# Attention weights copied within SBUF and transposed as fp32r, with the transposes and the value products two items behind their scores

## The chip, the cores and the metric

The kernel runs on one core of a Trainium2 chip. The metric is the device time of one execution in microseconds (us); lower is better. Before the change the median of three runs is 2031.01 us (2028.89 to 2032.45). A difference under about 0.2% (4 us) can't be told from no change here.

## The reference

One encoder layer is applied to two sequences of 1024 tokens and width 1024 (a prompt and a sample), and then a final RMS norm. Each token is normalised, scaled and shifted, and projected to a query latent (256), a key/value latent (128), a rotary key (64) and 512 Fourier channels. Four attention heads and a 2-D Fourier transform run side by side; their outputs share one projection, and a SwiGLU feed-forward part with 2816 hidden units follows. The part that the change touches is the softmax and the product with the values:

```python
sc = (jnp.einsum('bqhd,bkhd->bhqk', qn_b, k_nope)
      + jnp.einsum('bqhr,bkr->bhqk', qp_b, k_pe)).astype(jnp.float32) * scale
p = jax.nn.softmax(sc, axis=-1).astype(v.dtype)
return jnp.einsum('bhqk,bkhd->bqhd', p, v)
```

## The kernel before

**Arithmetic.** All data is fp32. Large products run on TensorE in the type fp32r. A number is split into a rounded high part, made by a copy on ScalarE, and the rest, made by a subtraction on VectorE (`split`, L61 to L63). A product is then three matmuls: high by high, high by low, low by high (`mm3`, L82 to L85).

**Stages.** The program runs through input projections, Fourier transforms, attention with the output projection and the second norm, and then the feed-forward part. The attention stage is one loop (from L1296) over 64 items and four closing steps. An item is one sequence `s`, one block `b` of 256 tokens, one head `h` and one half `u` of 128 query rows: 2 x 4 x 4 x 2. One pass `k` of the loop does, in the order of the program text:

- `scores` of item `k`: the product with the 1024 keys into two PSUM banks, the row maximum on VectorE (L1206), its scaling to a bias `nb` (L1207), the exponential with its sum on ScalarE (L1209), the reciprocal (L1210) and the scaling of the 128 x 1024 tile `p` (L1211). Two pairs of banks take turns. `p` has three buffers.
- on some passes, work on the queries: the rotary part for the next block (`rope_q`, `rope_flip`), and the absorbed query of the next head (`absorb_q`). Their tiles `hv` (two buffers) and `qa` (three buffers) are in the pool `e`.
- on every fourth pass (`k % 4 == 1`) `values`: 24 matmuls of the last four items' transposed weights with the values.
- `flip_p` of item `k - 1`: eight 128 x 128 transposes of `p` on TensorE, in the type fp32, four to a PSUM bank, and each bank split to fp32r parts `pt`. Two banks (`tbank`) take turns; the transposes of the normalised rows (`flip_h`, tile `pht`) and of the rotary queries (`rope_flip`, tile `pqt`) use the same two.
- `out_step`, which spreads the output projection, the second norm and its transposes of an earlier block over the passes.
- small jobs from the table `todo`, such as loading and splitting the output weights (`wv_load`, `wv_split`).

**What sets the order.** The text gives each instruction a rank. A planner with a model of the instructions' costs then writes the order of each engine's queue: among the instructions that it believes ready, the one that stands first in the text goes first. So in the trace a group of transposes often stands in the middle of a later item's score product. Once written, each queue runs strictly in its order, and an instruction whose input is late holds up all that is behind it. SyncE (SP) issues nearly all DMAs and is such a queue too. The rotary transposes of L858 read fp32r tiles already; those of L1157 and L1225 read fp32.

Of the kernel before, what the change touches and what calls it, by code (L numbers as in the profile page):

```python
# [12 lines left out]
F32 = mybir.dt.float32  # L13
F32R = mybir.dt.float32r
# [7 lines left out]
P = 128  # L22
D = 1024
N = 1024
# [28 lines left out]
def hybrid_encoder_kernel(ctx: ExitStack, tc: tile.TileContext, a: dict):  # L53
    nc = tc.nc
# [3 lines left out]
    def rd(t):  # L58
        return t.bitcast(F32)

    def split(hi, lo, src):  # L61
        here["a"] = nc.scalar.copy(hi, src).ins  # L62
        here["v"] = nc.vector.tensor_tensor(out=lo, in0=src, in1=rd(hi), op=ALU.subtract).ins  # L63
# [27 lines left out]
    ident = const.tile([P, P], F32, name="ident")  # L91
    make_identity(nc, ident)
    identr = const.tile([P, P], F32R, name="identr")
# [81 lines left out]
    with ExitStack() as st:  # L175
        p1b = st.enter_context(ExitStack())
        w2 = p1b.enter_context(tc.tile_pool(name="p1b", bufs=1, side="right", reuse_waits="tile"))
        w = st.enter_context(tc.tile_pool(name="p1", bufs=1, reuse_waits="tile"))
# [617 lines left out]
    S = {}  # L796
# [9 lines left out]
            nc.gpsimd.dma_start(fo_d[s][bs, gs], xs[s][bs, gs], accum_op=ALU.add)  # L806

    def half(name):
        return e.tile([P, 512], F32, tag="hv", name=name, bufs=2)

    def load_seq(s, lat):
        ckv = [e.tile([P, 8, KVL], F32R, tag=f"ckv{i}", name=f"ckv{i}", bufs=1) for i in range(2)]
# [16 lines left out]
        return e.tile([P, HEADS, P], F32R, tag="qp", name="qp", bufs=4)  # L829

    def qa_tiles():
        return [e.tile([P, 256], F32R, tag=f"qa{i}", name=f"qa{i}", bufs=3) for i in range(2)]

    def rope_q(s, b, u, bankf):
        ql = S["q", s, b]
# [57 lines left out]
    with ExitStack() as st:  # L893
        early = st.enter_context(ExitStack())
        wa = early.enter_context(tc.tile_pool(name="p2a", bufs=1, reuse_waits="tile"))
        w = st.enter_context(tc.tile_pool(name="p2", bufs=1, side="right", reuse_waits="tile"))
# [175 lines left out]
        for s in range(2):  # L1072
            for n in range(8):
                g, j = n // 4, (1, 2, 3, 0)[n % 4]
# [14 lines left out]
                if s == 1 and n == 0:  # L1089
# [3 lines left out]
                    e = E3.enter_context(tc.tile_pool(name="p3e", bufs=1, side="left", reuse_waits="tile"))  # L1093
# [20 lines left out]
    def tbank(name, dt=F32):  # L1114
        return tl_ps.tile([P, 4, P], dt, tag="t", name=name, bufs=2)
# [48 lines left out]
    def out_step(s, b, i):  # L1164
        if i in (9, 11):
            out_load(s, b, i // 2 - 4)
        if i in (10, 12, 15, 16):
            n = (10, 12, 15, 16).index(i)
            out_proj(s, b, n // 2, n % 2)
        if i in (12, 16):  # L1170
            norm2(s, b, i // 4 - 3, tl, True)
        if i in (14, 19):
            flip_h(s, b, int(i == 19))

    with ExitStack() as st:
# [7 lines left out]
        def scores(s, b, h, u):  # L1183
            lat = S[s][0]
            qa, qp = S["qa", s, b, h], S["qp", s, b, u]
            us = slice(u * P, u * P + P)
            ps = score_bank() if u == 0 else S.pop("ps")
            for g in range(2):
                gs = slice(512 * g, 512 * g + 512)
                o = ps[:, gs]  # L1190
                nc.tensor.matmul(o, qa[0][:, us], lat[0][:, 0, gs], start=u == 0, stop=False)
                nc.tensor.matmul(o, qa[0][:, us], lat[1][:, 0, gs], start=False, stop=False)
                nc.tensor.matmul(o, qa[1][:, us], lat[0][:, 0, gs], start=False, stop=False)
                nc.tensor.matmul(o, qp[:, h, :], lat[0][:, 1, gs], start=False, stop=u == 1)
            if u == 0:
                pn, qn = score_bank(), S["qp", s, b, 1]
                for g in range(2):
                    gs = slice(512 * g, 512 * g + 512)
                    nc.tensor.matmul(ps[:, gs], qp[:64, h, :], lat[1][:64, 1, gs], start=False, stop=True)
                    nc.tensor.matmul(pn[:, gs], qn[64:, h, :], lat[1][64:, 1, gs], start=True, stop=False)  # L1200
                S["ps"] = pn
            mx = tiny.tile([P, 1], F32, name="mx")
            nb = tiny.tile([P, 1], F32, name="nb")
            sm = tiny.tile([P, 1], F32, name="sm")
            rr = tiny.tile([P, 1], F32, name="rr")
            nc.vector.tensor_reduce(out=mx, in_=ps, axis=AX.X, op=ALU.max)  # L1206
            here["nb"] = nc.vector.tensor_scalar(out=nb, in0=mx, scalar1=-SCALE, scalar2=None, op0=ALU.mult).ins  # L1207
            p = w.tile([P, N], F32, tag="p", name="p", bufs=3)
            here["exp"] = nc.scalar.activation(p, ps, AF.Exp, bias=nb, scale=SCALE, accum_out=sm).ins  # L1209
            nc.vector.reciprocal(rr, sm)  # L1210
            nc.vector.tensor_scalar(out=p, in0=p, scalar1=rr[:, 0:1], scalar2=None, op0=ALU.mult)  # L1211
            S["p", s, b, h, u] = p
            S["rr"] = rr

        def flip_p(s, b, h, u):
            p = S.pop(("p", s, b, h, u))
            if h % 2 == 0 and u == 0:
                S["pt", s, b, h // 2] = [[w.tile([P, 4, 4, P], F32R, tag=f"pt{k}{g}", name=f"pt{k}{g}", bufs=1) for k in range(2)]
                                         for g in range(2)]
            i = 2 * (h % 2) + u  # L1220
            for g in range(2):
                pth, ptl = S["pt", s, b, h // 2][g]
                pt = tbank("ppt")
                for c in range(4):
                    nc.tensor.transpose(pt[:, c, :], p[:, (4 * g + c) * P : (4 * g + c + 1) * P], ident)  # L1225
                split(pth[:, :, i, :], ptl[:, :, i, :], pt)

        def values(s, b, q):
            ckv = S[s][1]
            pts = S.pop(("pt", s, b, q))  # L1230
            if q == 0:
                S["o", s, b] = [tl.tile([P, HEADS, 256], F32R, tag=f"o{i}", name=f"o{i}b{s}{b}", bufs=3) for i in range(2)]
            o = [t[:, 2 * q : 2 * q + 2, :].rearrange("p h t -> p (h t)") for t in S["o", s, b]]
            po = gbank()
            for c in range(8):
                pth, ptl = (t[:, c % 4].rearrange("p i t -> p (i t)") for t in pts[c // 4])
                mm3(po, ckv[0][:, c, :], ckv[1][:, c, :], pth, ptl, c == 0, c == 7)
            split(o[0], o[1], po)

        items = [(s, b, h, u) for s in range(2) for b in range(4) for h in range(HEADS) for u in range(2)]  # L1240
        nit = len(items)
# [31 lines left out]
        def wv_split(i):  # L1273
            h, g = i % 4, i // 4
            gs = slice(512 * g, 512 * g + 512)
            with tc.issue_after(here["nb"]), tc.issue_after(here["exp"]):
                split(wv[0][:, h, gs], wv[1][:, h, gs], S.pop(("wv", h, g)))

        todo = {k: [] for k in range(nit)}
# [3 lines left out]
            todo[34 + 3 * g].append(lambda g=g: gate_half(1, g))  # L1283
            todo[34 + 3 * g].append(lambda g=g: wv_load(1, g))
        for i in range(8):
            todo[39 + i // 2].append(lambda i=i: wv_split(i))
            todo[3 + i].append(lambda i=i: wv_split(i))
        for c, k in enumerate((49, 51, 57, 59)):
            todo[k].append(lambda c=c: comb_h(0, c))
# [6 lines left out]
        for k in range(nit + 4):  # L1296
            if k >= nit:
                i = k - nit
                out_proj(1, 2, i // 2, i % 2)
                S["tail", i] = here["v"]  # L1300
                if i == 1:
                    norm2(1, 2, 0, tl)
                    S["tail", 5], S["tail", 6] = here["n"]
            if k < nit:
                s, b, h, u = items[k]
                scores(s, b, h, u)
                if "scale" in S:
                    with tc.issue_after(here["nb"]):
                        S.pop("scale")()
                if k == nit - 1:  # L1310
                    with tc.issue_after(here["exp"]):
                        nc.scalar.activation(tiny.tile([P, 1], F32, tag="pc", name="warm"), cmask[:, 0:1], AF.Silu)
                nxt = items[k + 8 - k % 8] if k + 8 - k % 8 < nit else None
                i = k % 8
                if nxt is not None:
                    if i == 0:
                        load_q(*nxt[:2])
                    if i == 3 and nxt[1] == 0:
                        load_seq(nxt[0], [w.tile([P, 2, N], F32R, tag=f"lat1{i}", name=f"lat1{i}") for i in range(2)])
                    if i in (3, 4):  # L1320
                        rope_q(*nxt[:2], i - 3, gbank)
                    if i in (5, 6):
                        rope_flip(*nxt[:2], i - 5, tbank("pqt", F32R))
                if u == 1 and k + 1 < nit:
                    absorb_q(*items[k + 1][:3], gbank)
            if (k % 4 == 1 and 5 <= k < nit) or k == nit + 2:
                values(*divmod(k // 8 - (k % 8 == 1), 4), k // 4 % 2 ^ 1) if k < nit else values(1, 3, 1)
                if k == nit + 2:
                    S["tail", 4], S["tail", 7] = here["v"], here["a"]
            if 0 <= k - 1 < nit:  # L1330
                flip_p(*items[k - 1])
                if k == nit:
                    S["tail"] = here["a"], here["v"]
            for n in (k // 8 - 1, k // 8 - 2):
                if 0 <= n < NOUT:
                    out_step(*divmod(n, 4), k - 8 * n)
            for f in todo.get(k, ()):
                f()

# [640 lines left out]
```

## Time and profile before

| what | value |
|---|---|
| median of three runs | 2031.01 us |
| the profiled execution's own time | 2031.3 us |
| its span, first to last instruction | 2029.5 us |
| mean granted TensorE clock | 0.994 |
| DMA traffic | 370.33 MB, 182 GB/s on average |

The time of the profiled execution is 1.8 us longer than its span and 0.3 us longer than the median. The attention stage lies between about 302 and 722 us of the span. Matmul durations in the profile overlap, because matmuls are pipelined: what one of them costs is read from the distance between the starts of neighbours, not from its own duration. The engines are TensorE (PE, and its weight loads PEld), VectorE (DVE), ScalarE (ACT), GpSimd (POOL) and SyncE (SP, shown as SPq).

### The profile page before, as it was taken

The page shows a single profiled execution, that of the slowest core. Times are in us where ns is not written, and L with a number is a line of the kernel's source. Part 1 is how long each engine was busy: PE and PEld are TensorE (multiplying, and loading weights), DVE is VectorE, ACT ScalarE, POOL GpSimd, SP SyncE. Part 2 cuts the span into 40 slices and gives each one's busy share as a digit, 9 for nine tenths or more (in the row PEclk, how much of TensorE's full clock was granted, in tenths as well). Part 3 has the DMA queues.
Part 4 walks back from the last instruction along what each step waited for, and adds up shares of the span by engine and source line. Part 5 has one row for each costly group of instructions (what it writes and reads, how often), then busy time and mean ns, then how long its engine had stood idle before and what let it go on. Part 6 is the DMA issues. An engine that isn't in the chain of part 4 may idle for free.

```text
span 2029.5 us, 28291 instructions
## 1 busy us (share of the span) xinstructions
PE 1984.2 (98%) x9840; PEld 1624.1 (80%) x9840; DVE 1407.3 (69%) x2088; ACT 896.9 (44%) x1733; POOL 830.1 (41%) x1013
## 2 busy tenths in 40 slices
PE   8899999999999999999999999999999999999997
PEld 7788877888777777888888888877788888888876
DVE  5667757766677679878677577687755655657674
ACT  4555545555555564333333365453333333336441
POOL 2454123112313227879779411233654555510142
PEclk9999999999999999999999999999999999999999
DMA  9685793445542575645655587674422322357662
GB/s 376 207 289 171 255 346 102 125 94 130 138 122 94 178 269 187 207 163 192 206 166 190 178 304 249 219 234 147 141 93 102 116 93 103 116 184 270 229 224 89
DMA packets 181963, 370.33 MB, mean 182 GB/s; under 512 B 18556, under 2 KB 58236, under 8 KB 177724
## 3 DMA queue, kind: packets, MB, share of 16 engines
q1 hardware_dynamic: 163148, 310.71, 45.8%
q0 software_dynamic: 18672, 57.81, 9.5%
q8 instruction: 77, 1.26, 0.3%
q14 instruction: 66, 0.54, 0.1%
HBM read 256.46 MB, written 120.39 MB: 186 GB/s over the span
## 4 chain that ended last, share of the span: by engine, by line
PE 54%; DVE 2%; DMA 2%; POOL 1%; issue 1%; ACT 1%; SPq 0%; DVEq 0%; ACTq 0%; POOLq 0%
PE bank L84 18%; PE bank L83 18%; PE bank L85 18%; DVE wl L63 1%; DMA draw<-s_d 1%; POOL val L143 1%; DVE val L143 1%; ACT wh L62 0%; DMA val<-x_d 0%; DMA draw<-t_d 0%; DVE val L1777 0%; POOL rs_y L110 0%; DMA rgu<-in_wgu_dram 0%; DVE val L1751 0%; DVE val L140 0%
## 5 line engine op out<-in xcount | busy, mean ns | idle before, releaser
L83 PE MATMUL bank<-H,wh 128*128 128x512 f32 x1224 | 477.3, 390 | 5.1 <-DVE val L143 5.1
L85 PE MATMUL bank<-H,wl 128*128 128x512 f32 x1224 | 476.3, 389 | 0.2 <-DVE wl L63 0.2
L84 PE MATMUL bank<-H,wh 128*128 128x512 f32 x1224 | 476.2, 389 | 0.0
L143 DVE TENSOR_TENSOR val<-bank,val 128x512 f32<-128x512 f32 x244 | 166.8, 688 | 169.9 <-PE bank L85 167.2
L83 PEld LDWEIGHTS bank<-H,wh 128*128 128x128 f32 x1224 | 229.8, 188 | 55.6 <-DVE val L143 7.0
L85 PEld LDWEIGHTS bank<-H,wl 128*128 128x128 f32 x1224 | 229.8, 188 | 49.2 <-DVE wl L63 1.1
L84 PEld LDWEIGHTS bank<-H,wh 128*128 128x128 f32 x1224 | 229.8, 188 | 47.3
L63 DVE TENSOR_TENSOR wl<-draw,wh 128x512 fp32r<-128x512 f32 x286 | 201.3, 739 | 83.0 <-ACT wh L62 82.4
L62 ACT CAST wh<-draw 128x512 fp32r<-128x512 f32 x286 | 168.6, 621 | 157.9 <-PE bank L84 86.8
L84 PE MATMUL bank<-wl,wh 128*128 128x512 f32 x572 | 223.6, 391 | 2.5 <-DVE wl L63 2.5
L143 POOL TENSOR_TENSOR val<-val 128x512 f32<-128x512 f32 x58 | 83.1, 1441 | 344.9 <-DVE val L1751 188.7
L85 PE MATMUL bank<-wh,wl 128*128 128x512 f32 x572 | 222.6, 389 | 0.0
L83 PE MATMUL bank<-wh 128*128 128x512 f32 x572 | 222.6, 389 | 0.0
L62 ACT CAST wh<-rgu 128x512 fp32r<-128x512 f32 x171 | 106.5, 624 | 249.1 <-PE bank L84 193.8
L63 DVE TENSOR_TENSOR wl<-val,wh 128x512 fp32r<-128x512 f32 x133 | 132.4, 997 | 75.5 <-ACT wh L62 75.4
L63 DVE TENSOR_TENSOR wl<-rgu,wh 128x512 fp32r<-128x512 f32 x171 | 168.1, 984 | 5.8 <-ACT wh L62 5.8
L62 ACT CAST wh<-val 128x512 fp32r<-128x512 f32 x133 | 82.4, 623 | 178.7 <-PE bank L84 162.8
L140 POOL TENSOR_TENSOR val<-rgu 128x512 f32<-128x512 f32 x80 | 113.1, 1414 | 96.4 <-DMA rgu<-in_wgu_dram 92.6
L84 PEld LDWEIGHTS bank<-wl,wh 128*128 128x128 f32 x572 | 107.4, 188 | 27.7 <-DVE wl L63 5.5
L83 PEld LDWEIGHTS bank<-wh 128*128 128x128 f32 x572 | 107.4, 188 | 22.7 <-ACT wh L62 0.2
L85 PEld LDWEIGHTS bank<-wh,wl 128*128 128x128 f32 x572 | 107.4, 188 | 21.7
L140 POOL TENSOR_TENSOR val<-val 128x512 f32<-128x512 f32 x89 | 119.4, 1358 | 1.3
(393 smaller groups left out, 3919.9 us busy)
## 6 DMA issues: line engine op xcount, KB each, us to landing
rgu<-in_wgu_dram SPq DMA_DIRECT2D x86, 512.0 KB
draw<-s_d SPq DMA_DIRECT2D x143, 256.0 KB
s_d<-val POOLq DMA_DIRECT2D x88, 256.0 KB, 3.9
draw<-t_d SPq DMA_DIRECT2D x88, 256.0 KB
s_d<-val SPq DMA_DIRECT2D x66, 256.0 KB
wada<-in_wa_dram SPq DMA_DIRECT2D x16, 1024.0 KB
draw<-in_w_down_dram SPq DMA_DIRECT2D x55, 256.0 KB
xt<-in_x_dram SPq DMA_DIRECT2D x16, 512.0 KB
```

The lines of the kernel that those rows point to most:

```text
L62: here["a"] = nc.scalar.copy(hi, src).ins
L63: here["v"] = nc.vector.tensor_tensor(out=lo, in0=src, in1=rd(hi), op=ALU.subtract).ins
L83: nc.tensor.matmul(out, lh, rh, start=first, stop=False, skip_group_check=cont)
L84: nc.tensor.matmul(out, lh, rl, start=False, stop=False, skip_group_check=cont)
L85: here["pe"] = nc.tensor.matmul(out, ll, rh, start=False, stop=last, skip_group_check=cont).ins
L140: return eng.tensor_tensor(out=out, in0=x, in1=y, op=ALU.subtract).ins
L143: return eng.tensor_tensor(out=out, in0=x, in1=y, op=ALU.add).ins
```

## The change

After the scaling of `p`, a DMA on SyncE's queue copies the tile (128 partitions of 4 KB, 512 KB) to a new tile `pr` in SBUF whose type is fp32r. The bits are copied as fp32, so no rounding takes place. The transposes read `pr`, with the fp32r identity, into a PSUM tile of type fp32r, whose bits are read as fp32 by the split, as before. The transposes of an item move from one pass behind its scores to two, `values` from `k % 4 == 1` to `k % 4 == 2`, and `out_step` by one pass. Eight `wv_split` jobs move by one pass as well. Buffers: `p` from three to two, the new `pr` has two, `hv` from two to one, `qa` from three to two.

```diff
     def half(name):
-        return e.tile([P, 512], F32, tag="hv", name=name, bufs=2)
+        return e.tile([P, 512], F32, tag="hv", name=name, bufs=1)
...
     def qa_tiles():
-        return [e.tile([P, 256], F32R, tag=f"qa{i}", name=f"qa{i}", bufs=3) for i in range(2)]
+        return [e.tile([P, 256], F32R, tag=f"qa{i}", name=f"qa{i}", bufs=2) for i in range(2)]
...
-            p = w.tile([P, N], F32, tag="p", name="p", bufs=3)
+            p = w.tile([P, N], F32, tag="p", name="p", bufs=2)
             here["exp"] = nc.scalar.activation(p, ps, AF.Exp, bias=nb, scale=SCALE, accum_out=sm).ins
             nc.vector.reciprocal(rr, sm)
             nc.vector.tensor_scalar(out=p, in0=p, scalar1=rr[:, 0:1], scalar2=None, op0=ALU.mult)
-            S["p", s, b, h, u] = p
+            pr = w.tile([P, N], F32R, tag="pr", name="pr", bufs=2)
+            nc.sync.dma_start(rd(pr), p)
+            S["p", s, b, h, u] = pr
...
-                pt = tbank("ppt")
+                pt = tbank("ppt", F32R)
                 for c in range(4):
-                    nc.tensor.transpose(pt[:, c, :], p[:, (4 * g + c) * P : (4 * g + c + 1) * P], ident)
-                split(pth[:, :, i, :], ptl[:, :, i, :], pt)
+                    nc.tensor.transpose(pt[:, c, :], p[:, (4 * g + c) * P : (4 * g + c + 1) * P], identr)
+                split(pth[:, :, i, :], ptl[:, :, i, :], rd(pt))
...
-            todo[39 + i // 2].append(lambda i=i: wv_split(i))
+            todo[40 + i // 2].append(lambda i=i: wv_split(i))
...
-            if (k % 4 == 1 and 5 <= k < nit) or k == nit + 2:
-                values(*divmod(k // 8 - (k % 8 == 1), 4), k // 4 % 2 ^ 1) if k < nit else values(1, 3, 1)
+            if (k % 4 == 2 and 6 <= k < nit) or k == nit + 2:
+                values(*divmod(k // 8 - (k % 8 == 2), 4), k // 4 % 2 ^ 1) if k < nit else values(1, 3, 1)
...
-            if 0 <= k - 1 < nit:
-                flip_p(*items[k - 1])
-                if k == nit:
+            if 2 <= k <= nit + 1:
+                flip_p(*items[k - 2])
+                if k == nit + 1:
                     S["tail"] = here["a"], here["v"]
             for n in (k // 8 - 1, k // 8 - 2):
                 if 0 <= n < NOUT:
-                    out_step(*divmod(n, 4), k - 8 * n)
+                    out_step(*divmod(n, 4), k - 1 - 8 * n)
```

## The prediction

> **What bounds the kernel now.** I read the page first, for the busiest engine and the chain of work that ended last.
>
> ```profile
> PE 1984.2 (98%) x9840; PEld 1624.1 (80%) x9840; DVE 1407.3 (69%) x2088; ACT 896.9 (44%) x1733; POOL 830.1 (41%) x1013
> ...
> PE 54%; DVE 2%; DMA 2%; POOL 1%; issue 1%; ACT 1%; SPq 0%; DVEq 0%; ACTq 0%; POOLq 0%
> ```
>
> TensorE is busy in 98% of the span, and the chain that sets the end runs over it. The change acts on the attention stage alone, so I asked for that stretch (busy time by stretch, then the groups by line within it). The columns of the first row are the stretch, its length, and the busy time of each engine; at the end stand the granted clock, the DMA share and GB/s.
>
> ```profile
> 302.00:722.00 420.00, 410.87 (x2248) 329.94 (x2248) 294.63 (x538) 229.22 (x469) 97.39 (x156) 0.99 0.48 132
> ...
> L1225 PE MATMUL ppt<-ident,p 128*128 128x128 f32 x512 | 73.0, 279 | 3.3 <-DVE nb L1207 1.9 <-DVE pt L63 0.9 <-ACT ht L1160 0.5
> ```
>
> In the stage, too, TensorE is the bound: 410.87 of 420 us, VectorE 294.63 (70%), ScalarE 229.22. So time taken from its queue comes off the end, if nothing else holds it up. The DMA engines are busy for 0.48 of the stage, so there is room for copies. The 512 transposes of `p` (L1225) cover 73.0 us, but matmuls overlap, so their cost has to be read from starts.
>
> **The cheaper transposes.** The timeline has eight fp32r transposes in a row (L858) and eight fp32 ones (L1225), both between 512-wide matmuls. The columns are the start and the time from first start to last end.
>
> ```profile
> 296.73 0.81 PE L858 MATMUL pqt<-identr,qsk 128*128 128x128 f32 x8
> 297.38 0.47 PE L83 MATMUL bank<-wm,A 128*128 128x512 f32 x1
> 297.68 0.40 PE L84 MATMUL bank<-wm,A 128*128 128x512 f32 x1
> ...
> 309.52 1.04 PE L1225 MATMUL ppt<-ident,p 128*128 128x128 f32 x8
> 310.31 0.48 PE L1192 MATMUL ps_s<-lat,qa 128*128 128x512 f32 x1
> 310.63 0.39 PE L1193 MATMUL ps_s<-lat,qa 128*128 128x512 f32 x1
> 310.86 0.40 PE L1194 MATMUL ps_s<-lat,qp 128*128 128x512 f32 x1
> ```
>
> A 512-wide matmul takes 0.23 us from start to start (310.63 to 310.86). From the first transpose to the second matmul behind the group, less that 0.23, the fp32r group takes 297.68 - 296.73 - 0.23 = 0.72 us, and the fp32 group 310.63 - 309.52 - 0.23 = 0.88. That is 0.16 us an item, and 64 x 0.16 = **10.2 us** less on the bounding engine. Groups that are broken into two fours I count the same. The two ends of this price: nothing (the type doesn't matter for unrounded bits), and twice as much if the waits beside the transposes go too, which come next.
>
> The Trainium skill ("TensorE: Matmul & The Clock Gate", Part 4: PE-mode transpose) says that a transpose of about 275 ns is mostly the access latency to SBUF. By that the type would change little and the gain would be near zero, which is the third rival below. The row's mean of 279 ns agrees as a duration, but the starts are 0.72 against 0.88 us a group apart, and I follow those.
>
> **The waits beside them.**
>
> ```profile
> PEld ppt L1225 <- ACT ht L1160: 6.7, 17, 0.8
> PEld ppt L1225 <- issue: 6.4, 12, 2.3
> ...
> PE ps_s L1191 <- ACT qa L62: 2.8, 1, 2.8
> ```
>
> The columns are the sum, the times and the longest. The transposes wait for a PSUM bank that `pht` holds (6.7 us in sum on the weight-load side, partly covered by matmuls in flight). A faster group reaches such a wait earlier, which gives nothing; on the other hand the `pht` transposes of the second norm now fall on passes 4 and 7 of each eight instead of 3 and 6, and so no longer on a pass with `pqt`. I take 0, between +3 and -6 us.
>
> **The copy.** It adds 64 DMAs of 512 KB. No row shows a copy within SBUF, so I bound it by the nearest rows: one 256 KB load on the same queue, and two kinds on GpSimd's queue (last column: us to landing).
>
> ```profile
> 510.33 0.32 SPq L1244 DMA_DIRECT2D gah<-ga_d  x1
> ...
> 513.68 5.03 POOL L1270 TENSOR_TENSOR wvr<-wvr,gah 128x512 f32<-128x512 f32 x4 [3.38 <-DMA gah<-ga_d]
> ...
> fo_d<-in_x_dram POOLq DMA_DIRECT2D x16, 512.0 KB, 7.5
> ...
> hc_d<-hcb POOLq DMA_DIRECT2D x4, 1024.0 KB, 9.2
> ```
>
> The load of 256 KB is used 513.68 - 510.33 = 3.35 us after its issue; 1024 KB land after 9.2; the line between them gives 5.3 at 512 KB. The lower end is 3.35, the upper 7.5 (an accumulating transfer of the same size). I take **5 us**, nearest to the plain load. The Trainium skill ("DMA: Bandwidth & Descriptors", Where 436 GB/s comes from) says that a copy within SBUF is bound by the fabric at 435 GB/s, not by HBM. By that 512 KB move in an estimated 1.2 us, and the copy would land before the lower end; the sum would then lose its term for late copies.
>
> **What hides the copy.** With one more pass between scores and transposes, item k is turned about where item k+1 was turned before. I paired the 64 scalings (L1211) with the transposes of the next item. Those 63 distances are the slack for the copy. Here are the first and the last (items 0 and 62), which are also the two shortest:
>
> ```profile
> 308.42 0.74 DVE L1211 TENSOR_SCALAR p<-p,rr 128x1024 f32<-128x1024 f32 x1
> ...
> 312.41 0.81 PE L1225 MATMUL ppt<-ident,p 128*128 128x128 f32 x6
> ...
> 716.13 0.75 DVE L1211 TENSOR_SCALAR p<-p,rr 128x1024 f32<-128x1024 f32 x1
> ...
> 720.50 0.60 PE L1225 MATMUL ppt<-ident,p 128*128 128x128 f32 x4
> ```
>
> They are 312.41 - 309.16 = 3.25 us and 720.50 - 716.88 = 3.62; the next is 5.46, and the middle one of the 63 is 10.5. A copy of 5 us is late twice, by 1.75 and 1.4 us: **+3.1 us**, at the stage's start and end, where little else can fill TensorE's queue. At 3.35 us it is late once, by 0.1; at 7.5 us eight times, by 16.6 us in sum. If the planner knows the copy's length, it puts other matmuls first and part of this goes. I leave it in.
>
> **Buffers.** With two buffers the exponential of item k+2 needs item k's copy landed. The shortest distance from scaling to that exponential is item 7 to 9:
>
> ```profile
> 348.06 0.74 DVE L1211 TENSOR_SCALAR p<-p,rr 128x1024 f32<-128x1024 f32 x1
> ...
> 354.57 1.12 ACT L1209 ACTIVATE p<-ps_s,nb 128x1024 f32<-128x1024 f32 x1 [1.57 <-DVE nb L1207]
> ```
>
> 354.57 - 348.80 = 5.77 us, so 5 us fit: 0, and at 7.5 us 3.9 us over four items. Queued behind that exponential are ScalarE's copies of `pt`, which TensorE's value products need. `pr` needs its transposes two items back done, which is near the scaling of the item that reuses it; a copy waits there some 3 us and keeps later DMAs on SP back, mostly loads made early: 0. `hv` with one buffer holds the second `rope_q` until the first is split, which stands earlier on the same VectorE queue; `qa` with two is enough for the head in use and the next. I take 0 for both, up to 2 us before the first scores, where no transposes fill in.
>
> **Moved passes.** `values`, `out_step` and the transposes move together, so their distances stay. The closing steps have one transpose group more after the last scores, with four output projections to fill; its lateness is in the 3.1. A new order from the planner may move other waits by about 3 us either way.
>
> **Sum.** 2031.3 (the profiled execution) - 10.2 + 3.1 = 2024.2 us. That execution lies 0.3 us over the median; I round to **2024.0 us**.
>
> **The rivals.**
>
> *First, the gain is swallowed.* TensorE runs its transposes sooner and then waits for banks, copies or `qa` in about the same measure. Against a bound at 98% it needs 6 us or more of new waits: late copies at some 6.5 us landing (about 10 us in sum) do it, or the start, where the row of `qa` shows TensorE waiting 2.8 us already. Time 2030 us. For it: the two tight places. Against it: a slack of 10 us in the middle.
>
> *Second, slower: the copy stands in SP's queue behind a DMA that waits.* SP spends long times so.
>
> ```profile
> 461.95 0.33 SPq L1120 DMA_DIRECT2D x<-fo_d  x1
> 480.98 1.77 SPq L1162 DMA_DIRECT2D h_d<-ht  x2
> ...
> SPq L1162 <- ACT ht L1160: 108.4, 18, 18.7
> ```
>
> Between 461.95 and 480.98 SP issued nothing, since the store of `ht` at its head waited for ScalarE. A copy behind it would land late, and TensorE, in order, would stop at the transposes. It decides from about 5 us of hold (slack 10 less 5). If the planner misjudges one such store in each of the seven blocks by 8 us, that costs 7 x (8 - 5) = 21 us: 2024 + 21 = 2045 us. Against it: the store's releaser and the copy's both come from the score loop, so the planner sees their order as it is; where VectorE releases both, its own queue fixes it.
>
> *Third, the transposes get no cheaper*, because the bits are not rounded values: 2031.3 + 3.1 = 2034 us. For it: the only fp32r transposes in the trace read rounded tiles. Against it: nothing in the rows ties the distance to the bits.
>
> *Fourth, more than expected:* bank waits go as well (6 us) and no copy is late: 2015 us.
>
> **How the numbers follow.** A difference under 0.2% (4.1 us, so 2027 to 2035 us) can't be told from no change here. Forecast (2017 to 2027): 0.54. Fourth rival: 0.07. First (2027 to 2033): 0.22. Third: 0.05. Second: 0.12. Faster by over 0.2%: 0.54 + 0.07 = 0.61. Within: 0.22 + 0.05 = 0.27. Slower: 0.12. The range is 2016.5 to 2033.5 us: it reaches from the forecast's lower end over the first rival and leaves out the second, most of the third and much of the fourth, about 0.2.
>
> **What would show it.** Groups of eight L1225 transposes 0.65 us apart from first to next start, where now it is 0.79: right for the first term. The row of the copy's consumers: waits of L1225 for DMA `pr` of about 3 us in sum, at the two ends of the stage; tens of us would be the second rival, with SP's waits just ahead of them. ScalarE's L1209 waiting for DMA means that `p` lacks its third buffer. The stage's busy time of VectorE should stay at 294 us. I am wrong if the stage shrinks by less than 4 us, or if most of the loss lies outside it.

## The result and the profile after

The changed kernel takes **2049.16 us** (median of 4 runs, 2048.40 to 2053.28) where the kernel before takes 2031.12 on the same chip: the ratio is 1.0094, with a 95% interval of 1.0077 to 1.0112. It is slower by about 19 us. The prediction was 2024.0, faster, and the time lies outside its range of 2016.5 to 2033.5.

The top of the page and the chain of work that ended last, of the changed kernel:

```profile
span 2046.7 us, 28591 instructions
...
PE 1984.9 (97%) x9840; PEld 1620.8 (79%) x9840; DVE 1425.1 (70%) x2088; ACT 894.8 (44%) x1733; POOL 829.5 (41%) x1013
...
PE 54%; DVE 3%; DMA 2%; POOL 1%; issue 1%; ACT 0%; SPq 0%; DVEq 0%; ACTq 0%; POOLq 0%
```

TensorE is as busy as before (1984.9 us against 1984.2), but the span is 17.2 us longer. So the loss is idle time or slower clock, and the question is where. Busy time by stretch, over the whole attention stage (from the first score product to the first product behind the stage), first of before, then of after:

```profile
302.00:747.00 445.00, 434.17 (x2358) 348.95 (x2358) 313.27 (x561) 245.90 (x494) 105.34 (x177) 0.99 0.48 136
```

```profile
305.00:764.00 459.00, 432.55 (x2359) 345.09 (x2358) 315.04 (x562) 244.57 (x494) 102.97 (x177) 0.97 0.65 202
```

The stage grew by 14 us. TensorE stood idle in it for 459.00 - 432.55 = 26.4 us, before for 445.00 - 434.17 = 10.8: 15.6 us more. The granted clock fell from 0.99 to 0.97, and the DMA engines' share of busy time rose from 0.48 to 0.65. Behind the stage nothing changed: from there to the end it is 1282.3 us, before 1282.1. The stage also starts 3.1 us later. What TensorE waited for is in the view of the waits (sum, times, longest):

```profile
PE ppt L1227 <- DMA pr<-p: 19.3, 7, 6.8
...
ACT p L1209 <- DMA pr<-p: 9.1, 3, 6.6
```

The new wait of the transposes (L1227) for the copy sums to 19.3 us, in seven places; six of them, at 321, 350, 380, 542, 653 and 710 us, are over 1 us. ScalarE waited 9.1 us for copies too, since an exponential has to write a `p` that is still being copied. And the transposes themselves did become cheaper. In the timeline of TensorE a group of eight is now followed at this distance:

```profile
420.94 0.80 PE L1227 MATMUL ppt<-identr,pr 128*128 128x128 f32 x8
421.58 0.47 PE L1191 MATMUL ps_s<-lat,qa 128*128 128x512 f32 x1
```

From 420.94 to 421.58 are 0.64 us; in the prediction's rows the same distance was 310.31 - 309.52 = 0.79.

Now one of the late copies. The timeline around item 50's, with its scaling, SP's and GpSimd's DMA issues and the transposes that read the copy (the row of the copy, x2, is merged with that of item 51's copy, issued at 645.11):

```profile
636.25 1.59 DVE L1211 TENSOR_SCALAR p<-p,rr 128x1024 f32<-128x1024 f32 x1
...
640.38 0.81 SPq L1252 DMA_DIRECT2D hca<-h_d  x2
...
640.65 0.69 POOL L1262 DMA_DIRECT2D hc_d<-hcb  x1 [0.30 <-POOL hcb L140]
...
641.29 0.38 SPq L1120 DMA_DIRECT2D x<-fo_d  x1
...
641.84 3.75 SPq L1213 DMA_DIRECT2D pr<-p  x2
...
651.14 1.26 POOL L143 TENSOR_TENSOR hcb<-hca 128x512 f32<-128x512 f32 x1 [7.16 <-DMA hc_d<-hcb]
...
652.62 0.85 PE L1227 MATMUL ppt<-identr,pr 128*128 128x128 f32 x8 [3.16 <-DMA pr<-p]
```

The scaling ended at 637.84, but the copy was issued 4.0 us later: at the head of SP's queue stood the load of `hca`, which waited for GpSimd and went out at 640.38. Ahead of the copy were issued two halves of `hca` and a load of `x` on SP's own queue and a store of `hc_d` on GpSimd's, all within 1.5 us. The copy, issued at 641.84, is used at 652.62: **10.8 us**, where I had taken 5. The store landed just as late: GpSimd waited for it until 651.14. In before the same loads of `hca` and the same store were issued at 631.94 and 632.22. Busy time by stretches of 4 us from 2 us after that on, first of before, then of after (the DMA share is next to last):

```profile
634.00:638.00 4.00, 4.00 (x19) 3.27 (x18) 3.13 (x7) 1.93 (x4) 0.00 (x0) 1.00 0.94 283
638.00:642.00 4.00, 4.00 (x29) 3.68 (x28) 2.71 (x8) 1.91 (x5) 1.24 (x2) 1.00 0.45 192
642.00:646.00 4.00, 2.06 (x14) 1.22 (x12) 4.00 (x5) 0.91 (x2) 2.43 (x2) 1.00 0.02 4
```

```profile
642.00:646.00 4.00, 4.00 (x26) 3.44 (x25) 3.36 (x11) 2.81 (x6) 0.73 (x1) 1.00 0.94 271
646.00:650.00 4.00, 3.46 (x19) 2.31 (x17) 2.58 (x4) 0.00 (x0) 0.00 (x0) 1.00 0.99 408
650.00:654.00 4.00, 1.38 (x11) 1.32 (x12) 0.81 (x5) 0.83 (x2) 2.86 (x3) 1.00 0.53 216
```

In before, too, the DMA engines are full for a while (0.94), though the stage's mean is 0.48. It was room enough for the loads, but the copies of two items now stand in the same burst, and it lasts some 4 us longer.

In the other places of over 1 us from 350 us on, issue to use is 8.7, 11.0, 13.1 and 10.1 us, each time just behind loads of `lat`, `ckv`, `x` or `hca`. The first, at 321 us, stood behind two loads of 256 KB (`gah`, `wvr`) and took 4.6.

### The profile page after: what moved, and what is told of

It reads as the page before. It is cut to its first block, busy times and chain, and to the rows that moved or that the text cites. A ratio compares the mean times of both kernels' runs of the same rounds, so it can differ in the third digit from the quotient of the medians.

```text
span 2046.7 us, 28591 instructions
## 1 busy us (share of the span) xinstructions
PE 1984.9 (97%) x9840; PEld 1620.8 (79%) x9840; DVE 1425.1 (70%) x2088; ACT 894.8 (44%) x1733; POOL 829.5 (41%) x1013
## 4 chain that ended last, share of the span: by engine, by line
PE 54%; DVE 3%; DMA 2%; POOL 1%; issue 1%; ACT 0%; SPq 0%; DVEq 0%; ACTq 0%; POOLq 0%
PE bank L84 18%; PE bank L83 18%; PE bank L85 18%; DVE wl L63 1%; DVE val L143 1%; DMA val<-x_d 0%; DMA draw<-s_d 0%; ACT wh L62 0%; POOL val L143 0%; DVE val L1779 0%; DMA rgu<-in_wgu_dram 0%; POOL rs_y L110 0%; DMA draw<-t_d 0%; DMA draw<-in_w_down_dram 0%; DVE val L140 0%
## 5 line engine op out<-in xcount | busy, mean ns | idle before, releaser
L63 DVE TENSOR_TENSOR wl<-val,wh 128x512 fp32r<-128x512 f32 x133 | 145.3, 1094 | 69.5 <-ACT wh L62 69.3
```

## The experiments

The theory was that the **copies come late**, because of the loads that share DMA queues and engines with them, and that TensorE and ScalarE then wait. An expectation may call it A1 where it concerns what shares SP's queue. The rivals: the **move** by one pass costs the time by itself, the **smaller buffers** do, or the **traffic** of the copies delays other transfers. Each part was taken alone. In the table "stage" is the time from the first score product to the first product behind the stage, and "idle" the sum of TensorE's idle times in it; both are worked out from the trace.

| kernel | time, us | ratio to before, 95% | stage | idle |
|---|---|---|---|---|
| before | 2031.1 | 1 | 445.3 | 10.8 |
| after | 2049.2 | 1.0094 [1.0077, 1.0112] | 459.2 | 26.4 |
| type_only | 2021.7 | 0.996 [0.9947, 0.9972] | 437.8 | 11.2 |
| small_buffers | 2032.2 | 1.0009 [0.9993, 1.0024] | 442.0 | 8.4 |
| move_only | 2037.0 | 1.0037 [1.0024, 1.005] | 446.8 | 9.7 |
| move_big_buffers | 2035.1 | 1.0028 [1.0018, 1.0038] | 452.2 | 11.3 |
| no_copy | 2030.4 | 1.0002 [0.9989, 1.0016] | 445.1 | 13.7 |
| type_move_big_buffers | 2032.7 | 1.0013 [1.0004, 1.0022] | 447.3 | 13.7 |
| dummy_copy | 2039.3 | 1.0053 [1.0036, 1.007] | 451.9 | 14.3 |
| half_copy | 2044.6 | 1.0081 [1.0066, 1.0096] | 457.8 | 24.6 |
| copy_pool_queue | 2057.4 | 1.0145 [1.0128, 1.0162] | 464.8 | 28.1 |
| copy_act_queue | 2050.5 | 1.0096 [1.0068, 1.0123] | 463.0 | 21.6 |
| loads_pool_queue | 2038.5 | 1.0053 [1.0037, 1.0069] | 451.1 | 17.6 |
| one_pass | 2108.4 | 1.0386 [1.0367, 1.0406] | 522.9 | 66.9 |

The kernels are compared by their ratios, since before itself stood between 2028.3 and 2031.1 us in the four jobs.

### The change without the copy

VectorE's scaling writes the fp32r tile itself, so the weights are rounded there, which the changed kernel doesn't do. Order, type and small buffers stay as in the change.

```diff
-            nc.vector.tensor_scalar(out=p, in0=p, scalar1=rr[:, 0:1], scalar2=None, op0=ALU.mult)
             pr = w.tile([P, N], F32R, tag="pr", name="pr", bufs=2)
-            nc.sync.dma_start(rd(pr), p)
+            nc.vector.tensor_scalar(out=pr, in0=p, scalar1=rr[:, 0:1], scalar2=None, op0=ALU.mult)
```

> The changed kernel without the copy: the scaling on VectorE writes the fp32r tile itself, so the weights are rounded to fp32r and their low parts are lost. Type, order and buffers are those of the change. Theory A (the copies land late, behind bulk transfers): TensorE's waits for the copy (19.3 us in the profile of the change) and the slow clock after them go, what stays is the cheaper transposes (-10 us against before) and some 3 us ahead of the first scores: about 2024 us. Theory B (the move by one pass makes the waits): about 2045 us, with waits of the transposes in other names.

Measured: 1.0002. The copy with all that follows from it is worth 1.0094 - 1.0002 = 0.92%, **18.7 us** (about 14 to 23 by the two intervals): nearly the whole loss. But without it the kernel isn't faster than before either, so something else eats the gain of the transposes.

### The type alone

The kernel before in its order and with its buffers; only the scaling writes a rounded tile, and the transposes are fp32r (`p` then needs one buffer, `pr` two).

```diff
-            p = w.tile([P, N], F32, tag="p", name="p", bufs=3)
+            p = w.tile([P, N], F32, tag="p", name="p", bufs=1)
...
-            nc.vector.tensor_scalar(out=p, in0=p, scalar1=rr[:, 0:1], scalar2=None, op0=ALU.mult)
-            S["p", s, b, h, u] = p
+            pr = w.tile([P, N], F32R, tag="pr", name="pr", bufs=2)
+            nc.vector.tensor_scalar(out=pr, in0=p, scalar1=rr[:, 0:1], scalar2=None, op0=ALU.mult)
+            S["p", s, b, h, u] = pr
...
```

(The lines of the transposes are those of the change.)

> The kernel before with fp32r transposes alone: VectorE's scaling writes an fp32r tile (weights rounded, low parts lost), transposes one pass behind as before, hv and qa with their old buffers. If the distance between starts in the profile carries over (0.16 us an item), 2021 us; if waits for PSUM banks swallow it, 2030 us.

Measured: 0.996 of before, which is 8.1 us less (5.7 to 10.8 by the interval). This version beats both kernels: the type needs no copy if the scaling may round.

### The move alone, with small and with large buffers

The changed kernel with its copy and its fp32r transposes taken out again:

```diff
             nc.vector.tensor_scalar(out=p, in0=p, scalar1=rr[:, 0:1], scalar2=None, op0=ALU.mult)
-            pr = w.tile([P, N], F32R, tag="pr", name="pr", bufs=2)
-            nc.sync.dma_start(rd(pr), p)
-            S["p", s, b, h, u] = pr
+            S["p", s, b, h, u] = p
...
-                    nc.tensor.transpose(pt[:, c, :], p[:, (4 * g + c) * P : (4 * g + c + 1) * P], identr)
+                    nc.tensor.transpose(pt[:, c, :], p[:, (4 * g + c) * P : (4 * g + c + 1) * P], ident)
```

Here `p` has four buffers, `hv` one and `qa` two (move_only), or three, two and three (move_big_buffers).

> The move by one pass alone: fp32 transposes straight from p, no copy, p with four buffers, hv with one and qa with two as in the change. Theory A: the move costs nothing beyond the small buffers, 2031 to 2035 us. Theory B: 2045 us or more.

> The move alone (turns and values two items behind, fp32 transposes, no copy), with the buffers of before (p 3, hv 2, qa 3). move_only was the same with p 4, hv 1, qa 2, and stood at 1.0037 of before (2036.95 us in its job). If the smaller buffers cost some 2 us by themselves (small_buffers: 1.0009, not resolved), this kernel stands near 2034, ratio about 1.0025, and the 2 us wait of the qsk transposes at the start of the stage is gone from its trace. If the move itself is the whole loss, it stands where move_only does, 1.0037. If the buffers were the whole loss, it stands at 1.000. Either way the last of the eight rounds of eight items (first score of a round to first score of the next; the last one to the last score) should stay near 49 to 52 us where before has 42.8, if that loss belongs to the move.

Both are slower than before: 1.0037, and 1.0028 with before's buffers, that is **+5.7 us** (3.7 to 7.7). So the order costs time by itself. The intervals of the two overlap. In their traces the last eight items, from the first score product of the first to the last one of the last, take 49.6 us (move_only) and 52.7 (move_big_buffers), where before has 42.8; the expectation had 49 to 52. The buffers were also taken alone, as before with `hv` one and `qa` two:

```diff
-        return e.tile([P, 512], F32, tag="hv", name=name, bufs=2)
+        return e.tile([P, 512], F32, tag="hv", name=name, bufs=1)
...
-        return [e.tile([P, 256], F32R, tag=f"qa{i}", name=f"qa{i}", bufs=3) for i in range(2)]
+        return [e.tile([P, 256], F32R, tag=f"qa{i}", name=f"qa{i}", bufs=2) for i in range(2)]
```

> The kernel before with hv at one buffer and qa at two, nothing else. The profile of the change has its first score matmul 3.1 us later than before (305.2 against 302.1 us) behind a wait of 2.2 us for the rotary queries. Theory C (the single hv buffer makes that wait): about 2034 us. Else: 2031 us.

1.0009, with 1 inside the interval: no cost that can be told. The expectation's 3 us ahead of the first score product are there in the trace (306.4 us, before 302.1), but type_only, which keeps the large buffers, has them too (305.9). So the later start of the stage in after is not shown to come from the buffers; its cause stays open. The move and the type together, with large buffers, are the check of both:

```diff
-        return e.tile([P, 512], F32, tag="hv", name=name, bufs=1)
+        return e.tile([P, 512], F32, tag="hv", name=name, bufs=2)
...
-        return [e.tile([P, 256], F32R, tag=f"qa{i}", name=f"qa{i}", bufs=2) for i in range(2)]
+        return [e.tile([P, 256], F32R, tag=f"qa{i}", name=f"qa{i}", bufs=3) for i in range(2)]
...
-            p = w.tile([P, N], F32, tag="p", name="p", bufs=2)
+            p = w.tile([P, N], F32, tag="p", name="p", bufs=1)
```

(shown against no_copy.)

> The move and the type together, no copy (the scaling writes the rounded tile, so the weights are rounded there), with hv 2 and qa 3. no_copy was the same with hv 1 and qa 2 and stood at 1.0002 of before; type_only, without the move, at 0.996. If move and type simply add, with buffers costing 2 us: about 2028, ratio 0.999. If the buffers cost nothing: 1.0002 as no_copy. If the buffers are what no_copy lost against type_only: 0.996.

1.0013, not better than no_copy with 1.0002. The buffers of `hv` and `qa` are ruled out as the cause: large ones did not bring back what no_copy lost against type_only (0.996 to 1.0002, 8.5 us).

Where the move loses it can be seen by dividing the stage into rounds of eight items, by the starts of their first score products. In no_copy the first seven rounds together take 4.0 us less than in type_only. The last one takes 52.3 us instead of 41.9. It now also holds the transposes and values that were put off, and there is little else to mix with them. Three short idle times stand there. The timeline of TensorE in no_copy, then the busy time by stretch, of before and twice of no_copy, the second time right behind the three idle times:

```profile
697.51 0.53 PE L1226 MATMUL ppt<-identr,pr 128*128 128x128 f32 x4 [0.84 <-ACT ht L1160]
698.91 0.53 PE L1226 MATMUL ppt<-identr,pr 128*128 128x128 f32 x4 [0.86 <-ACT ht L1160]
700.26 0.50 PE L1191 MATMUL ps_s<-lat,qa 128*128 128x512 f32 x1 [0.82 <-ACT qa L62]
```

```profile
696.00:708.00 12.00, 11.04 (x55) 8.08 (x55) 7.69 (x14) 6.97 (x16) 5.64 (x5) 1.00 0.56 149
```

```profile
696.00:708.00 12.00, 9.47 (x29) 5.75 (x29) 6.29 (x11) 5.18 (x14) 5.90 (x5) 0.70 0.79 248
```

```profile
701.00:711.00 10.00, 10.00 (x22) 6.60 (x23) 3.35 (x7) 1.39 (x3) 1.99 (x2) 0.50 0.97 356
```

In the same 12 us no_copy executed 29 matmuls, before 55: TensorE idled 2.5 us instead of 1.0, and its granted clock was 0.70 instead of 1.00. From 701 to 711 us TensorE was busy throughout at a clock of 0.50; its 512-wide matmuls start 0.43 us apart there (707.09 to 707.52), against 0.23 at full clock. By that the clock cost about 5 us, an estimate from this one trace. So of the 10.4 us by which the last round is longer, about 5 are clock and 1 is idle time; the remaining 4 are what the first seven rounds gained. In move_only the place is less clear: its stage is only 1.5 us longer than that of before, and of the 7.2 us by which its span is longer, 4.3 lie behind the stage.

### The copy's traffic alone

The kernel small_buffers, with a copy of each `p` that nobody reads:

```diff
             nc.vector.tensor_scalar(out=p, in0=p, scalar1=rr[:, 0:1], scalar2=None, op0=ALU.mult)
+            pr = w.tile([P, N], F32, tag="pr", name="pr", bufs=1)
+            nc.sync.dma_start(pr, p)
             S["p", s, b, h, u] = p
```

> The kernel before with small buffers (hv one, qa two) and a copy of each scaled tile to a tile that nothing reads; transposes in fp32 straight from p, one pass behind. Theory A (the copies cost because TensorE waits for them): 2032 us, as with the small buffers alone. If the traffic itself slows other loads or engines: 2036 us or more.

It costs 1.0053 - 1.0009 = 0.44%, some 9 us; by the medians of the two jobs 7. Nobody waits for the copied data here, so this is the traffic and the place in SP's queue. In the traces the loss stands in two places, the fifth round (60.4 us, in small_buffers 55.3) and the part behind the last score product (38.3, in small_buffers 33.0). The timeline shows the path in the first; the second was not followed up. First small_buffers, then dummy_copy:

```profile
514.72 5.04 POOL L1270 TENSOR_TENSOR wvr<-wvr,gah 128x512 f32<-128x512 f32 x4 [3.24 <-DMA gah<-ga_d]
...
521.84 0.75 DVE L1143 TENSOR_SCALAR xn<-x,rs_r 128x1024 f32<-128x1024 f32 x1 [5.54 <-POOL rs_r L114]
```

```profile
518.05 1.29 POOL L1272 TENSOR_TENSOR wvr<-wvr,gah 128x512 f32<-128x512 f32 x1 [3.57 <-DMA gah<-ga_d]
...
524.89 0.75 DVE L1143 TENSOR_SCALAR xn<-x,rs_r 128x1024 f32<-128x1024 f32 x1 [9.01 <-POOL rs_r L114]
...
527.78 1.97 PE L1227 MATMUL ppt<-ident,p 128*128 128x128 f32 x8 [4.33 <-DVE pt L63]
```

The loads of `wvr`, with copies between them on SP's queue, come late: GpSimd's first product with them in this stretch starts at 508.19 us, in small_buffers at 504.88. The next piece of `gah` is issued only behind these products, 3.0 us later than in small_buffers, and GpSimd reaches the inverse root of the second norm late. VectorE's normalisation waits 9.01 us for that, the splits of `pt` stand behind it, and TensorE idles 4.33 us for their bank. In small_buffers TensorE waits 0.54 us there.

### Half the copy

VectorE scales in two halves and writes the second straight to `pr` (rounded); the DMA copies the first, 256 KB.

```diff
-            nc.vector.tensor_scalar(out=p, in0=p, scalar1=rr[:, 0:1], scalar2=None, op0=ALU.mult)
             pr = w.tile([P, N], F32R, tag="pr", name="pr", bufs=2)
-            nc.sync.dma_start(rd(pr), p)
+            nc.vector.tensor_scalar(out=p[:, :512], in0=p[:, :512], scalar1=rr[:, 0:1], scalar2=None, op0=ALU.mult)
+            nc.vector.tensor_scalar(out=pr[:, 512:], in0=p[:, 512:], scalar1=rr[:, 0:1], scalar2=None, op0=ALU.mult)
+            nc.sync.dma_start(rd(pr)[:, :512], p[:, :512])
```

> The change with a copy of half the size: the first 512 columns of the weights are copied (256 KB), the other half is written as fp32r by VectorE's scaling (rounded, low parts lost there). Theory A1 (the time in front of the copy counts, not its own): most of the 19 us of waits stay, 2042 to 2049 us. If the copy's own size makes it late: waits halve or better, 2035 us or less.

```profile
PE ppt L1228 <- DMA pr<-p: 15.4, 6, 5.3
```

1.0081: half the bytes takes away 4 us of the wait of 19.3 us (the row is from the waits), and the time can't be told from that of the whole copy (1.0094; the intervals overlap). What makes a copy late is mostly not its own length.

### Whose queue

Three kernels move the copies, or the loads, to another queue. First the copies to GpSimd's, then the copies to ScalarE's, then the loads of `x` and `hca` from SP's queue to GpSimd's, with the copies left on SP.

```diff
-            nc.sync.dma_start(rd(pr), p)
+            nc.gpsimd.dma_start(rd(pr), p)
```

> The change with the copy issued by GpSimd instead of SyncE; TensorE's order is the same but for 24 lines. In the change a copy is issued on SyncE's queue right behind loads of 512 KB and 1 MB and lands 8 to 13 us later. Theory A1 (it stands behind those loads in their queue): on another queue it takes turns with them, TensorE's waits for the copy fall from 19.3 us to under 6, about 2035 us. Theory A2 (the DMA engines are simply full then, whatever the queue): waits stay near 19 us, 2049 us. GpSimd's own waits may hold some copies back, which would add waits elsewhere.

```diff
-            nc.sync.dma_start(rd(pr), p)
+            nc.scalar.dma_start(rd(pr), p)
```

> The copy issued from ScalarE's queue in place of SP's. ScalarE ran the exponential that precedes the scaling, and its queue holds no bulk loads. If the lateness comes from DMA engines that are full while bulk loads run, as the run with the copy on GpSimd's queue suggested, the late copies stay (waits of the transposes for the copy 15 to 25 us in sum, landing 4 to 5 us undisturbed and 8 to 12 beside bulk loads), and ScalarE also waits at each copy's issue for the scaling: 2050 to 2065 us. If it were SP's queue that holds the copies, the waits fall under 8 us in sum and the time to about 2038.

```diff
-        nc.sync.dma_start(x2, fo_d[s][r0 : r0 + P, :])
+        nc.gpsimd.dma_start(x2, fo_d[s][r0 : r0 + P, :])
...
-                nc.sync.dma_start(A[:, 2 * i : 2 * i + 2, :], h2_d[s][:, c + 4 * i, :].rearrange("p (a b) -> p a b", a=2))
+                nc.gpsimd.dma_start(A[:, 2 * i : 2 * i + 2, :], h2_d[s][:, c + 4 * i, :].rearrange("p (a b) -> p a b", a=2))
```

> The change with the loads of the output blocks (x from fo_d, 512 KB) and of the combinations (hca from h_d, two of 512 KB) issued by GpSimd, the copies still by SyncE; TensorE's order is the same. Theory A1: the waits at the copies of items 50 and 58 (3.2 and 6.8 us in the change, right behind hca loads) go, those of items 6, 10 and 34 (behind loads of the keys and values) stay: about 2038 us. Theory A2: 2049 us.

The rows for the transposes' wait for the copy, in the view of the waits of the three kernels, in this order:

```profile
PE ppt L1227 <- DMA pr<-p: 22.3, 10, 6.6
```

```profile
PE ppt L1227 <- DMA pr<-p: 9.3, 5, 3.8
```

```profile
PE ppt L1227 <- DMA pr<-p: 11.3, 6, 3.3
```

GpSimd's queue is no cure (1.0145), but it isn't an empty queue either. It carries the store of `hc_d` and the accumulating transfers of `fo_d`, and there the copy stands behind these. The timeline of that kernel at the longest wait, and from its source view the time from issue to landing of all 64 copies:

```profile
698.18 0.64 POOL L1262 DMA_DIRECT2D hc_d<-hcb  x1 [0.30 <-DVE pt L63]
...
698.82 0.55 POOL L1213 DMA_DIRECT2D pr<-p  x1
...
709.25 0.98 PE L1227 MATMUL ppt<-identr,pr 128*128 128x128 f32 x6 [6.64 <-DMA pr<-p]
```

```profile
DMA to landing us min/median/max: 2.8/4.5/11.4
```

On ScalarE's queue, which carries no load, and with the loads taken off SP's, the sum about halves. The waits for items 34, 50 and 58 (542, 653 and 710 us in after, 13.6 us in sum) are gone in both. Others come in their place: 3.30 us for item 59 with the loads moved, and 1.32 and 3.79 us for items 59 and 61 on ScalarE's queue. The stage's DMA share is 0.67 in loads_pool_queue, no lower than after's 0.65. So for the late half of the stage **the queue that a copy shares** sets its lateness, in two ways: by what stands ahead of the copy among the transfers, and by the hold before the copy is issued at all. For item 34, held for only 0.6 us in after, it is the first: from issue to use it took 13.1 us there, with a wait, and 9.9 and 10.7 without one in the two kernels. For items 50 and 58 the two are not separated: their copies were issued 4.0 us behind the scaling in after and 3.5 us on GpSimd's queue, but 1.3 to 1.4 us in these two kernels. The waits near 350, 365 and 380 us stay in all three kernels. There the choice of queue is not the cause, and what is was not settled: the DMA share between 342 and 350 us is 0.92 in after, and item 6's copy is issued 2.7 us behind its scaling, because `pr` with its two buffers wasn't free.

Only loads_pool_queue gains (1.0053, 8 us less than after). On ScalarE's queue the fewer waits bring nothing (1.0096). That kernel's undisturbed rounds take 54.9 us where after's take 53.0, spread over small distances between matmuls which the trace doesn't count as idle, and the part behind the last score product 41.3 instead of 33.6, which holds the wait of 3.79 us for item 61. The time of 2050.5 us lies in the range that the expectation gave for full DMA engines, but with waits of 9.3 us and not 15 to 25, so it does not speak for that reason. ScalarE now has to hold at each copy's issue until the scaling is done; that this is the cause was not tried.

### One pass instead of two

The changed kernel, with turns and values one item behind, as before (the output steps and the eight `wv_split` jobs move back with them):

```diff
-            if (k % 4 == 2 and 6 <= k < nit) or k == nit + 2:
+            if (k % 4 == 1 and 5 <= k < nit) or k == nit + 2:
...
-            if 2 <= k <= nit + 1:
-                flip_p(*items[k - 2])
+            if 0 <= k - 1 < nit:
+                flip_p(*items[k - 1])
```

> The changed kernel with its turns and values one item behind their scores instead of two, the copy, the type and the small buffers kept. If the order that is written protects the copies, taking one pass away makes them late: by the distances from scaling to the own item's transposes in the profile of before (median 2.7 us) a copy of 4.4 us would come late 44 times, by 93 us in sum, and the planner could make up for perhaps half: 2095 us. If the planner, which knows the length of a copy, puts the transposes behind other matmuls by itself, the second pass buys little: within 8 us of the changed kernel, 2041 to 2057, with a similar sum of waits of the transposes for the copy (20 us).

```profile
PE ppt L1227 <- DMA pr<-p: 59.0, 19, 5.9
```

1.0386, some 78 us over before. The waits for copies are three times those of after. So the second pass is what makes the copy bearable, and the planner alone does not make up for it. It also gives a direct look at the landing: in the 19 places where TensorE waited, issue to use is 3.4 us at the least, 7.3 in the middle and 10.3 at the most.

## Why the prediction was wrong, point by point

**The failing step is the copy's landing.** The prediction took one time for all 64 copies, 5 us "nearest to the plain load", counted from the end of the scaling, and called the copy late twice: +3.1 us. Away from large loads that was about right: the first wait measured 4.6 us, and on GpSimd's queue the median is 4.5. But TensorE waits for the worst copies and not for the middle one, and those took 8.7 to 13.1 us from issue to use, and some were issued late as well. The lateness was 19.3 us in sum for TensorE and 9.1 for ScalarE. The lower bound was a load ahead of which SP had issued nothing for over 4 us, and the upper one a median of 16 transfers whose longest took 10.3 us. The stage's mean share of 0.48 was read as "room for copies". The estimate of 1.2 us for moving 512 KB lies below the shortest landing measured, 2.8 us. The loads come in bursts, with a share of 0.94 and 0.99 in the rows above, in before as in after. Also, the prediction's own working for 7.5 us gave 16.6 us of lateness, so 2031.3 - 10.2 + 16.6 = 2037.7 us, and its range ended below that.

The Trainium skill ("DMA: Bandwidth & Descriptors", Queues, rings and completion order) says that each DMA engine takes turns between the queues that have work for it. By that rule a copy waits for all that stands ahead in its own queue, and only shares with the others. The waits on ScalarE's queue and with the loads moved go the same way (9.3 and 11.3 us for 19.3), though the hold before the issue became shorter there too. What sharing the engines with other queues costs is not settled here.

**The cheaper transposes were right.** Forecast: 0.65 us from first to next start, and 10.2 us in sum. Measured: 0.64 us, and 8.1 us for the type alone (10.2 lies within its interval). The third rival falls: unrounded bits in after and rounded ones in type_only both run at the shorter distance.

**The moved passes were valued at 0, ±3, and cost 5.7 us** by themselves (8.5 on top of the type). The reason given, that `values`, `out_step` and the transposes keep their distances, looked at the middle of the stage. There it holds, and the early rounds even gain. What is put off piles up in the last round, where TensorE idled three times for 0.8 us and then ran at half the clock for 10 us. That it ran out of other work to fill these idle times with was argued from the program, not tried. The prediction asked what was late at the end only for the copy.

**The copy's effect on others was left out.** The traffic alone cost 7 to 9 us, by loads that then came late. The prediction counted only who reads the copy, and that it keeps "later DMAs on SP back, mostly loads made early: 0".

**Buffers.** `hv` and `qa` cost nothing that can be told, as forecast. Two buffers of `p` did make ScalarE wait, 9.1 us in three places (0 was taken, 3.9 at 7.5 us), which follows from the landing. Two buffers of `pr` held SP's copies, in ten places:

```profile
SPq L1213 <- PE ppt L1227: 14.5, 10, 2.9
```

**The second rival had the sign, and its mechanism in part.** It had the copy held in SP's instruction queue behind a DMA that waits, a store of `ht`. Of the 64 copies 39 were issued within 0.07 us of their scaling's end, and 17 more than 1 us behind it. Of the six copies with a wait of over 1 us, five were held: item 6's for 2.7 us until `pr` was free, items 10's and 34's for 1.1 and 0.6 us behind loads, and items 50's and 58's for 4.0 us each, behind a load of `hca` that waited for GpSimd. SP's row for that load:

```profile
SPq L1252 <- POOL hcb L140: 28.1, 3, 10.7
```

From issue to use these five took another 8.7 to 13.1 us. Had they been issued at the end of their scalings and taken as long from there, some 11 of the 19.3 us of waits would be gone: an estimate from the after trace, no run tried it. So the rival's time of 2045 us came near partly by luck: it had seven holds behind another store, and took the copy's own time as 5 us.

**The sum, again, by what was measured:** type -8.1, move and buffers on top +8.5, copy +18.7, together +19.1 us, of which the first two cancel. Of the copy's 18.7, the traffic alone is 7 to 9; the rest is waiting for the copies and the clock that the idle times cost. For the clock the traces give an estimate: at a granted clock of 0.50 TensorE was busy in the stage for 19.4 us in after, 13.7 in no_copy and 5.1 in before. Half of the difference to no_copy, some 3 us of the 18.7, is clock. Against before it is some 7 us: with 15.6 us more idle time, less the 8.1 of the transposes, that is 14.6 us, about the 14 by which the stage grew.

## What to carry to other kernels

A transfer that TensorE waits for in order has to be priced at its slowest place: look at what can hold its issue, at what is issued on its queue in the 2 us ahead of it and at the DMA share of the 10 us behind it, not at the stage's mean. Before a tile is copied only to change its type, look whether the engine that writes it can write that type: here the same transposes without the copy were 0.4% faster than before, and with it 0.9% slower. Work that is put off by a pass is not free if the loop ends: look for what fills TensorE in the last round.

## What the runs showed of the hardware that was not expected

- A copy of 512 KB from SBUF to SBUF took 2.8 us at the least, 4.5 in the middle and 11.4 at the most from issue to landing on GpSimd's queue, in one and the same kernel.
- Three idle times of TensorE of 0.82 to 0.86 us within 4 us were followed by a lower clock: 0.50 from 701 to 711 us in no_copy, 0.70 over 696 to 708 us with 9.47 of the 12 us busy, while before kept 1.00 with 11.04. The Trainium skill ("TensorE: Matmul & The Clock Gate", A second HAM failure mode: psum-queue depth-cycling) says that TensorE's short idle times between groups of matmuls can come often enough to make the clock drop and recover; these rows agree.
- fp32r transposes of bits that were never rounded start as close to each other as those of rounded ones (0.64 us for eight in after, and 425.66 - 425.03 = 0.63 in no_copy).

```profile
425.03 0.80 PE L1226 MATMUL ppt<-identr,pr 128*128 128x128 f32 x8
425.66 0.47 PE L1191 MATMUL ps_s<-lat,qa 128*128 128x512 f32 x1
```
